# A decoder block in split fp32: plain w_down rows inside the seven-product banks, paced loads, gate/up by features

## The chip, the cores and the metric

The kernel runs on one core of one Trainium2 chip. The time is the device time of one execution in microseconds; the time before is the median of three runs, 2729.72 us (2727.82 to 2730.57). TensorE (PE) multiplies 128x128 weight tiles with a moving operand, VectorE (DVE) and ScalarE (ACT) do elementwise work. GpSimd (POOL) and SyncE (SP) here do little but issue DMAs, each on a queue of its own.

## The reference

One layer of a decoder on 512 tokens and 2048 features in fp32: attention and a gated delta rule, merged by gates, then a SwiGLU channel mixer of 5632 features and a last norm. The change touches the mixer and what follows it alone:

```python
h = _rmsnorm(x, norm_ffn[l]) * (1.0 + sc_f) + sh_f
gate, up = jnp.split(h @ w_gate_up[l], 2, axis=-1)
x = x + gt_f * ((jax.nn.silu(gate) * up) @ w_down[l])
...
return _rmsnorm(x, final_norm)
```

## The kernel before

**Precision.** Each fp32 operand is split into a high and a low part (`hi`/`lo`, `h2h`/`h2l`, `xh`/`xl`, `ah`/`al`), and each product of tiles is three matmuls: high by high, and the two mixed ones. ACT makes the high part, DVE the low one.

**Order.** Every instruction is first recorded, so that all rows of the profile show one line, L482; then a planner with costs and due times reorders DVE and ACT. PE, SP and POOL keep the order in which the program was written. A `Driver` walks through `Unit`s: a unit loads a raw weight tile (`load`, SP's queue), splits it, runs its matmuls and then a closing step. `pump` moves side chains one step on after every twelve counts; a chain that yields n rests for n−1 of its turns. `side` issues on POOL's queue. Working tiles are 68 slots of 128x512 (`S`), raw weights take a ring of five, split ones four, and PSUM has eight banks.

**Gate/up.** `w_gate_up` has 22 pairs of 256-column sets. `gu_tokens(0, ...)` and `gu_tokens(1, ...)` compute sets s=0 and 1 with token tiles as weights and 512 weight columns moving. The results have tokens on partitions, so `gu_read` applies silu and product, and later `turned_a` turns them on PE (four transposes of a block, then a copy to `f_dram`). The other 20 sets go through `strassen`, the seven-product form (`big(1)` to `big(10)`).

**w_down.** Its 44 row blocks of 128 fall into three groups. Rows 0–15 and 16–31 go through `tokens_down(ks, n)`, the seven-product form: for ks=0, 1 and n=0, 1 (1024 columns each), sixteen units; eight with the products m1, m6, m7, m5 (`FIRST4`, 24 matmuls each), then eight with m2, m4, m3 (`LAST3`, 18 each), 336 matmuls in all. The products' weights are sums of weight tiles (`sums`), stored in `s_dram` by POOL in the first eight units and loaded again in the last eight. The moving-side parts in `down[ks]` come from `f_dram` through `sums_down`. The other rows, 32–43, are plain: 36–39 stay in slots (`aT`), 32–35 and 40–43 wait in `a_dram` (`kept_a`, `reload_a`).

**The end of the program, before.** In order: gate/up s=0 and 1, the ten seven-product sets, the plain rows 36–39 for all 2048 columns (`dn(36, n)`, whose `dn_done` puts the results into `down_dram`), `tokens_down(0,0)` and `(0,1)`, the plain rows 40–43, `tokens_down(1,0)` and `(1,1)`, and the last stage `last_dn` with the plain rows 32–35, the transposed residual `x2` and the final norm. Each set's results are added to `down_dram` by adding stores on POOL (`add_down`), as a side chain that the next set finishes first: `drv.finish(chains["out"])`. In `tokens_down(1,1)`, `at(i)` names what is loaded ahead of unit i: the `down_dram` tiles (`back_s`), gate rows, x2 (`back_x`) and `a_dram` tiles (`aT_back`), the last two on POOL's queue.

Of the kernel before, what the change touches and what calls it, by code (L numbers as in the profile page):

```python
# [16 lines left out]
P = 128  # L17
T = 512
NT = 4
# [472 lines left out]
def block_kernel(ctx: ExitStack, tc: tile.TileContext, a: dict, out):  # L492
# [1805 lines left out]
    def tokens_down(ks, n):  # L2298
# [64 lines left out]
        def after(c, t):  # L2363
            tt = lambda o, x, y, op=ALU.add: nc.vector.tensor_tensor(o, x, y[:], op)
            less = lambda o, x, y: nc.vector.scalar_tensor_tensor(o, x, -1.0, y[:], op0=ALU.mult, op1=ALU.subtract)
# [10 lines left out]
            elif c == "m2":  # L2376
                if final:
                    tt(s_t[t, 2][:], s_t[t, 2][:], ps["m1"][t])
                    ps["m1"][t] = None
                    return  # L2380
                x = S("g0")
                nc.scalar.copy(x[:], ps["m1"][t][:])
                tiles[0, t, 0] = x[:]
                ps["m1"][t] = None
            elif c == "m4":
                if final:
                    tt(s_t[2 + t, 2][:], s_t[2 + t, 2][:], ps["m7"][t])
                    ps["m7"][t] = None
                    return
                x = S("g1")  # L2390
                tt(x[:], v[t], ps["m7"][t])
                tiles[1, t, 0] = x[:]
                ps["m7"][t] = None
            else:
                if final:
                    tt(s_t[t, 3][:], s_t[t, 3][:], ps["m5"][t], ALU.subtract)
# [4 lines left out]
                ps["m5"][t] = None  # L2401

# [9 lines left out]
        def outputs(keys):  # L2412
            for h, t, f in keys:
                add_down(2 * h + t, 2 * n + f, tiles.pop((h, t, f)))
                yield 2

        def unit(i):
# [5 lines left out]
            for c, w, j, bank, x in products:  # L2423
                for t in range(2):
                    for m, (xi, wi) in enumerate(((0, 0), (0, 1), (1, 0))):
                        def one(c=c, w=w, j=j, bank=bank, x=x, t=t, m=m, xi=xi, wi=wi):
                            mm(ps[bank][t][:], x(q)[xi][:, 256 * kk + P * t:256 * kk + P * t + P], box["w"][w][wi][:, j, :],
                               start=i == 0 and m == 0, stop=k == 7 and m == 2, skip_group_check=True)
# [6 lines left out]
            def post():  # L2435
# [5 lines left out]
                if i == 15:  # L2441
                    if (ks, n) == (1, 0):
                        kept.update(tiles)
                    elif not final:
                        chains["out"] = drv.add(outputs([(1, 0, 1), (1, 1, 1), (0, 0, 0), (0, 1, 0), (1, 0, 0), (1, 1, 0), (0, 0, 1), (0, 1, 1)]))
# [3 lines left out]
        return [unit(i) for i in range(16)]  # L2449

    early, s_t, rows, kept = [], {}, [], {}
    down_dram = dram.tile([NT, P, D], F32, name="down_dram")

    def add_down(t, n, src, **kw):

        nc.gpsimd.dma_start(down_dram[t][:, 512 * n:512 * n + 512], src, accum_op=ALU.add)
# [97 lines left out]
    def sums_down(ks):  # L2554
# [3 lines left out]
        def free(q):  # L2558
            return q < 4 and gone[ks] >= min(q + 2, 4) and (q < 3 or plain_sets[0] > 4 * ks + 3)
# [9 lines left out]
        for q in range(4):  # L2569
# [10 lines left out]
            for c, dst, x, y, op in (("m7", "x7", "a11", "a21", ALU.subtract), ("m1", "a11", None, None, None),  # L2580
                                     ("m5", "a21", "a22", "a21", ALU.subtract), ("m4", "a22", None, None, None),
                                     ("m6", "a11", "a11", "a21", ALU.add), ("m2", "a12", None, None, None),
                                     ("m3", "a12", "a11", "a12", ALU.subtract)):
# [18 lines left out]
    first_tiles = {}  # L2602

    def gu_read(s, ht, bank):

        if s == 0:
            first_tiles[ht] = S("g0")
        o, g = first_tiles[ht][:, 256 * s:256 * s + 256], S("sl")
        nc.scalar.activation(g[:, 0:256], bank[:, 0:256], AF.Silu)
        nc.vector.tensor_tensor(o, g[:, 0:256], bank[:, 256:512], ALU.mult)  # L2610

    def gu_tokens(s, hts):

        banks = {}

        def unit(k0):
# [8 lines left out]
            def pre():  # L2625
                if k0 == 0:
                    for ht in hts:
                        banks[ht] = PS(f"gu{s}")

            def one(kk, h, t, n, xi, wi):  # L2630
# [3 lines left out]
                if k == KT - 1 and n == 2:  # L2634
                    gu_read(s, (h, t), banks.pop((h, t)))

            mms = [lambda kk=kk, h=h, t=t, n=n, xi=xi, wi=wi: one(kk, h, t, n, xi, wi)
                   for kk in range(2) for h, t in hts for n, (xi, wi) in enumerate(((0, 0), (0, 1), (1, 0)))]

            def post():  # L2640
                if k0 + 2 == KT and s == 1:
                    for q in range(4):
                        h2T[1][q] = None
                    turning.append((0, first_tiles))

            return Unit(start, split, mms, pre, post, weight=2, alone=s == 0, late=k0 + 2 == KT)
# [3 lines left out]
    def dn_done(n, k0):  # L2650
        def done(ps):
            for t in range(NT):
                y = S("y")
                nc.scalar.copy(y[:], ps[t][:])
                if k0 == 36:
                    side(down_dram[t][:, 512 * n:512 * n + 512], y[:])
                else:
                    add_down(t, n, y[:])
            plain_sets[0] += 1
            if n == 3:  # L2660
                for k in range(k0, k0 + 4):
# [5 lines left out]
    def ffn():  # L2667
        def gu0():
            us = []
            for h in range(2):  # L2670
                half = gu_tokens(0, [(h, t) for t in range(2)])
# [5 lines left out]
                us += half  # L2677
# [6 lines left out]
            with_pre(us, start)  # L2684
            return us
# [6 lines left out]
        def dn(k1, n):  # L2692
            us = tm_set(f"dn{k1}_{n}", lambda k0, nk: plain(w_dn, k1 + k0, nk, 512 * n, 512), 4,
                        lambda k: (aT[k1 + k][0][:], aT[k1 + k][1][:]), dn_done(n, k1))
# [3 lines left out]
        LAST = 32  # L2698
# [3 lines left out]
        def load_rows(src):  # L2702
            for i in range(4):
                r = S("row")
                load(r[:], src[512 * i:512 * i + 512].partition_broadcast(P))
                rows.append(r)

        def back_x(n):
            for h in range(2):
                for q in (2 * n, 2 * n + 1):  # L2710
                    x2[h][q] = S("x2")
                    side(x2[h][q][:], x2_dram[h, q])

        def back_s(n):
            for t in range(NT):
                s_t[t, n] = S("sd")
                load(s_t[t, n][:], down_dram[t][:, 512 * n:512 * n + 512])
# [78 lines left out]
        def last_dn():  # L2796
# [4 lines left out]
            def aT_back():  # L2801
                for k in range(4):
                    reload_a(LAST + k)

            def at(i):
                if i == 2:
                    back_s(0)
                elif i == 3:
                    with_kept(0)
                    back_s(1)  # L2810
                elif i == 4:
                    with_kept(1)
                    load_rows(g_dram)
                elif i == 5:
                    gated(0)
                elif i == 6:
                    gated(1)
                    back_s(2)
                elif i == 7:
                    back_x(0)  # L2820
                elif i == 8:
                    back_s(3)
                elif i == 9:
                    early[0]()
                    back_x(1)
                elif i == 11:
                    aT_back()
                elif i == 13:
                    back_x(2)
                elif i == 14:  # L2830
                    back_x(3)
                elif i == 15:
                    load_rows(a["final_norm"])

            for i, u in enumerate(tokens_down(1, 1)):
                u = begin(lambda i=i: at(i))(u)
                yield u

            for n in range(2):
                for k0 in (0, 2):  # L2840
                    yield last_weights(n, k0)
                    for t in range(NT):
                        u = token_unit(t, n, k0=k0, nk=2, free=t == 3)
                        if k0 == 2 and t == 0:
                            u = begin(lambda n=n: gated(2 + n))(u)
# [11 lines left out]
        both = gu_tokens(1, [(h, t) for h in range(2) for t in range(2)])  # L2857
        yield from with_pre(both, lambda: xc.append(drv.add(combine())))
# [9 lines left out]
        for n in range(4):  # L2868
            for k, u in enumerate(dn(36, n)):
                yield with_pre([u], more)[0]  # L2870
                if n in (1, 2):
                    yield Unit(mms=turned_a(2 * n + k - 2), pre=lambda: drv.finish(chains["act"]))
        for n in range(2):
            for i, u in enumerate(tokens_down(0, n)):
                if (n, i) == (1, 10):
                    def start():
                        for k in range(40, 44):
                            reload_a(k)
                        maker[1] = drv.add(sums_down(1))
                    with_pre([u], start)  # L2880
                yield u
        for n in range(4):
            for u in dn(40, n):
                yield with_pre([u], more)[0]
# [64 lines left out]
```

## Time and profile before

| what | us |
|---|---|
| median of three runs (range) | 2729.72 (2727.82 to 2730.57) |
| profiled execution | 2731.62 |
| its span | 2729.8 |
| gate/up s=0 and 1 | 1375.7 to 1464.6 |
| seven-product gate/up sets | 1464.6 to 2245.2 |
| plain rows 36–39 | 2245.2 to 2290.6 |
| tokens_down(0,0) and (0,1) | 2290.6 to 2451.7 |
| plain rows 40–43 | 2451.7 to 2495.3 |
| tokens_down(1,0) and (1,1) | 2495.3 to 2669.4 |
| last stage | 2669.4 to 2720.8 |

The stages are the times from the first matmul of one to the first of the next. In a row of windows, "PE busy (x673)" has the count of matmuls behind the busy time, which is modelled; the rate is better read from the stage's length and the count. PEclk is the share of the full clock that the throttle granted. In a DMA row the last number is the median time from issue to landing.

### The profile page before, as it was taken

The page shows a single profiled execution, that of the slowest core. Times are in us where ns is not written, and L with a number is a line of the kernel's source. Part 1 is how long each engine was busy: PE and PEld are TensorE (multiplying, and loading weights), DVE is VectorE, ACT ScalarE, POOL GpSimd, SP SyncE. Part 2 cuts the span into 40 slices and gives each one's busy share as a digit, 9 for nine tenths or more (in the row PEclk, how much of TensorE's full clock was granted, in tenths as well). Part 3 has the DMA queues.
Part 4 walks back from the last instruction along what each step waited for, and adds up shares of the span by engine and source line. Part 5 has one row for each costly group of instructions (what it writes and reads, how often), then busy time and mean ns, then how long its engine had stood idle before and what let it go on. Part 6 is the DMA issues. An engine that isn't in the chain of part 4 may idle for free. (4 is left out here: it accounts for less than half of the span.)

```text
span 2729.8 us, 37437 instructions
## 1 busy us (share of the span) xinstructions
PE 2695.4 (99%) x13518; PEld 2263.3 (83%) x13518; DVE 2124.8 (78%) x3257; ACT 1181.6 (43%) x1648; POOL 230.1 (8%) x363
## 2 busy tenths in 40 slices
PE   9999999999999999999999999999999999998998
PEld 7888788888888888889988888888888888877876
DVE  8985666776978887688797777788777787876878
ACT  4343432442345343244483444444444455444434
POOL 0000011102001000000000000000000102113020
PEclk9999999999999999999999999999999999999999
DMA  9995555645666889525864566566665667689692
GB/s 345 354 369 185 164 171 165 201 137 175 187 183 214 313 291 329 193 88 126 256 199 144 192 201 204 201 212 201 204 206 189 218 217 251 198 266 211 194 347 101
DMA packets 306690, 587.13 MB, mean 215 GB/s; under 512 B 42228, under 2 KB 81412, under 8 KB 306504
## 3 DMA queue, kind: packets, MB, share of 16 engines
q1 hardware_dynamic: 260920, 481.01, 53.5%
q0 software_dynamic: 26368, 76.85, 9.4%
q10 hardware_dynamic: 19216, 26.87, 2.8%
q8 instruction: 106, 1.74, 0.3%
q14 instruction: 80, 0.66, 0.1%
HBM read 497.58 MB, written 88.09 MB: 215 GB/s over the span
## 5 line engine op out<-in xcount | busy, mean ns | idle before, releaser
L482 ACT CAST hi<-raws 128x1024 fp32r<-128x1024 f32 (+2 forms) x360 | 325.5, 905 | 546.3 <-PE m L482 274.2
L482 DVE TENSOR_TENSOR lo<-raws,hi 128x1024 fp32r<-128x1024 f32 (+2 forms) x360 | 370.2, 1039 | 169.5 <-ACT hi L482 165.1
L482 ACT CAST hi<-raw 128x1024 fp32r<-128x1024 f32 (+2 forms) x259 | 268.5, 1038 | 475.3 <-DMA raw<-in_w_in_dram 79.4
L482 DVE TENSOR_TENSOR lo<-raw,hi 128x1024 fp32r<-128x1024 f32 (+2 forms) x259 | 313.1, 1210 | 170.4 <-ACT hi L482 168.5
L482 DVE CUSTOM_DVE_ANT_0 rawm<-rawm,cbc 128x1024 f32<-128x1024 f32 x192 | 233.2, 1229 | 24.1 <-DMA rawm<-in_w_mod_dram 23.7
L482 ACT CAST hi<-sums 128x1024 fp32r<-128x1024 f32 x136 | 142.8, 1051 | 144.2 <-PE m L482 120.8
L482 DVE TENSOR_TENSOR lo<-sums,hi 128x1024 fp32r<-128x1024 f32 x136 | 166.1, 1222 | 47.2 <-ACT hi L482 46.9
L482 PE MATMUL m<-hi,h2h 128*128 128x512 f32 x480 | 190.2, 396 | 0.0
L482 PE MATMUL m<-lo,xh 128*128 128x512 f32 x448 | 178.6, 399 | 9.2 <-DVE lo L482 8.9
L482 PE MATMUL m<-hi,h2l 128*128 128x512 f32 x480 | 187.2, 390 | 0.0
L482 PE MATMUL m<-lo,h2h 128*128 128x512 f32 x480 | 187.1, 390 | 0.0
L482 PE MATMUL m<-hi,xh 128*128 128x512 f32 x448 | 177.6, 396 | 9.3 <-ACT hi L482 9.3
L482 PE MATMUL m<-hi,xl 128*128 128x512 f32 x448 | 176.8, 395 | 0.0
L482 DVE TENSOR_TENSOR sums<-raws,raws 128x1024 f32<-128x1024 f32 x112 | 136.5, 1219 | 26.2 <-DMA s_dram<-raws 23.8
L482 POOL DMA_DIRECT2D s_dram<-raws x112 | 64.1, 578 | 690.5 <-DVE raws L482 680.6
L482 PEld LDWEIGHTS m<-lo,xh 128*128 128x128 f32 x448 | 85.6, 191 | 33.2 <-DVE lo L482 15.6
L482 PEld LDWEIGHTS m<-hi,xh 128*128 128x128 f32 x448 | 85.5, 191 | 29.5 <-ACT hi L482 11.6
L482 PEld LDWEIGHTS m<-hi,h2l 128*128 128x128 f32 x480 | 90.1, 188 | 18.9
L482 PEld LDWEIGHTS m<-lo,h2h 128*128 128x128 f32 x480 | 90.3, 188 | 17.7
L482 PEld LDWEIGHTS m<-hi,h2h 128*128 128x128 f32 x480 | 90.2, 188 | 17.5
L482 PE MATMUL gb<-hh,hi 128*128 128x512 f32 x256 | 101.9, 398 | 0.0
L482 PE MATMUL gb<-hl,hi 128*128 128x512 f32 x256 | 100.0, 390 | 0.0
(538 smaller groups left out, 7026.4 us busy)
## 6 DMA issues: line engine op xcount, KB each, us to landing
raws<-in_w_gate_up_dram SPq DMA_DIRECT2D x400, 256.0 KB, 3.5
rawm<-in_w_mod_dram SPq DMA_DIRECT2D x192, 512.0 KB, 5.5
raw<-in_w_in_dram SPq DMA_DIRECT2D x143, 512.0 KB, 4.6
raws<-in_w_down_dram SPq DMA_DIRECT2D x160, 256.0 KB, 4.9
s_dram<-raws POOLq DMA_DIRECT2D x112, 256.0 KB, 3.3
raws<-s_dram SPq DMA_DIRECT2D x112, 256.0 KB, 2.8
rawa<-in_w_in_dram SPq DMA_DIRECT2D x32, 512.0 KB, 3.8
raws<-in_w_o_dram SPq DMA_DIRECT2D x48, 256.0 KB, 3.1
```

What stands on the lines that cost most here:

```text
L482: self.tc.keep_in_program_order(op.call(*op.args, **op.kwargs))
```

## The change

**Gate/up by features.** Sets s=0 and 1 now take the weight tile as the stationary operand, with 256 tokens moving: 768 matmuls of 256 columns for 384 of 512. The results have features on partitions. `gu_done` stores them to `f_dram` directly; the sixteen transposes of `turned_a` for these sets, with their copies, go. On PE, at the first stage (`gu` are PSUM banks, `hi`/`lo` the split weights, `h2h`/`h2l` the split tokens), before:

```order
L482 MATMUL gu_2138_2278<-hi_2264,h2h_2250 128x512
L482 MATMUL gu_2138_2278<-lo_2265,h2h_2250 128x512
L482 MATMUL gu_2138_2278<-hi_2264,h2l_2251 128x512
L482 MATMUL gu_2139_2279<-hi_2264,h2h_2250 128x512
L482 MATMUL gu_2139_2279<-lo_2265,h2h_2250 128x512
L482 MATMUL gu_2139_2279<-hi_2264,h2l_2251 128x512
```

and on PE at the same place after:

```order
L482 MATMUL gu_2138_2278<-h2h_2250,hi_2264 128x256
L482 MATMUL gu_2138_2278<-h2l_2251,hi_2264 128x256
L482 MATMUL gu_2138_2278<-h2h_2250,lo_2265 128x256
L482 MATMUL gu_2139_2279<-h2h_2250,hi_2264 128x256
L482 MATMUL gu_2139_2279<-h2l_2251,hi_2264 128x256
L482 MATMUL gu_2139_2279<-h2h_2250,lo_2265 128x256
```

The operands have changed places, the width is halved, and in this stage a weight tile's matmuls go to four banks, one for each block of 128 features, where they went to two, one for each block of 128 tokens.

**Plain rows.** Rows 36–39 and 32–35 are now one group of eight (`ORDER`). For columns 0–1023 they are computed in front of `tokens_down(0,0)` (`dn(0)`, `dn(1)`, 192 matmuls). For columns 1024–2047 they follow `tokens_down(0,1)` as eight `plus_unit`s, again 192 matmuls, which add into that set's own PSUM banks; `with_plus` then reads the banks out once. Rows 40–43 take the place of 32–35 in the last stage. Rows 36–39 are stored to `a_dram` too.

**down_dram.** Before, 16 tiles are put and 32 added. After, 16 are put (`put_down`) and eight added, those of `tokens_down(0,0)`, as a chain that rests between its steps; `pre` sees to it that four are out by the eighth unit of the next set and all by the sixteenth. On POOL around the first half of `tokens_down(0,1)` (`raws` is a tile of weight sums, `euvw` and `g` are result tiles), before:

```order
L482 DMA s_dram<-raws_3947 128x512
L482 DMA s_dram<-raws_3953 128x512
L482 DMA s_dram<-raws_3961 128x512
L482 DMA down_dram<-euvw 128x512 x2
L482 DMA down_dram<-g_3823_3963 128x512
L482 DMA down_dram<-g_3824_3964 128x512
L482 DMA down_dram<-g_3825_3965 128x512
L482 DMA down_dram<-g_3826_3966 128x512
L482 DMA down_dram<-euvw 128x512 x2
L482 DMA s_dram<-raws_3972 128x512
```

and on POOL at the same place after:

```order
L482 DMA s_dram<-raws_3948 128x512
L482 DMA down_dram<-euvw 128x512
L482 DMA s_dram<-raws_3963 128x512
L482 DMA down_dram<-euvw 128x512
L482 DMA s_dram<-raws_3970 128x512
L482 DMA down_dram<-euvw 128x512
L482 DMA s_dram<-raws_3977 128x512
L482 DMA down_dram<-euvw 128x512
L482 DMA s_dram<-raws_3984 128x512
L482 DMA down_dram<-g_3799_3939 128x512
L482 DMA down_dram<-g_3800_3940 128x512
L482 DMA down_dram<-g_3801_3941 128x512
```

The first four adds now stand one at a time between the stores of weight sums; the `g` adds follow the last of these.

**Paced loads.** `reload_a` moves from POOL's queue to SP's, one row block (two tiles) per unit: 32–35 in the last units of `big(10)`, all eight of `ORDER` once more in the second half of `tokens_down(0,1)`, 40–43 in the last units of `tokens_down(1,1)`. There the loads ahead of the last stage are spread too, two per unit, all on SP; twelve of the sixteen x2 loads and the final norm's rows move into the last stage (`more_back`). On POOL in the second half of `tokens_down(1,1)` before:

```order
L482 DMA s_dram<-raws_4388 128x512
L482 DMA x_4277_4417<-x_dram 128x512
L482 DMA x_4278_4418<-x_dram 128x512
L482 DMA x_4279_4419<-x_dram 128x512
L482 DMA x_4280_4420<-x_dram 128x512
L482 DMA x_4297_4437<-x_dram 128x512
```

and on SP there after:

```order
L482 DMA raws_4389<-s_dram 128x512
L482 DMA raws_4389<-in_w_down_dram 128x512
L482 DMA raws_4390<-in_w_down_dram 128x512
L482 DMA x_4251_4391<-x_dram 128x512
L482 DMA x_4252_4392<-x_dram 128x512
L482 DMA raws_4397<-s_dram 128x512
L482 DMA raws_4397<-in_w_down_dram 128x512
```

The x2 loads have left POOL's queue and stand in pairs behind each unit's three weight loads.

**Signs.** A few differences are taken the other way round (`less`, `sums_down`), one instruction for one. The diff, cut to its core:

```diff
-        else:
-            for i in range(2):
-                side(a_dram[k - 32, i], hl[i][:].bitcast(F32))
+        for i in range(2):
+            side(a_dram[k - 32, i], hl[i][:].bitcast(F32))
...
         def pre(i):
             down_ready(ks, i % 8 // 2)
+            if i == 7:
+                while "out" in chains and sent[0] < 4:
+                    drv.step(chains["out"])
+            if i == 15 and "out" in chains:
+                drv.finish(chains["out"])
             if i == 0:
                 drv.ahead = 2
-                if "out" in chains:
-                    drv.finish(chains["out"])
...
+        def with_plus(f, t):
+            if f:
+                nc.vector.tensor_tensor(v[t], ps["m5"][t][:], v[t], ALU.subtract)
+                nc.vector.tensor_tensor(up1[t], up1[t], ps["m6"][t][:], ALU.add)
+                tiles[0, t, 1], tiles[1, t, 1] = v[t], up1[t]
+                ps["m5"][t] = ps["m6"][t] = None
+            else:
+                x, y = S("g0"), S("g1")
+                nc.scalar.copy(x[:], ps["m1"][t][:])
+                nc.vector.tensor_tensor(y[:], v[t], ps["m7"][t][:], ALU.add)
+                tiles[0, t, 0], tiles[1, t, 0] = x[:], y[:]
+                ps["m1"][t] = ps["m7"][t] = None
...
+            def one(kk, t, x, w, h):
+                bank = (("m1", "m7"), ("m5", "m6"))[f][t // 2]
+                mm(ps[bank][t % 2][:], aT[plus[k0 + kk]][x][:, tok(t)], box["w"][w][:, kk, :],
+                   start=(bank, k0 + kk, h) == ("m6", 0, 0), stop=(k0 + kk, h) == (7, 2), skip_group_check=True)
+                if (k0 + kk, h) == (7, 2) and t > 1:
+                    with_plus(f, t - 2)
...
-                add_down(2 * h + t, 2 * n + f, tiles.pop((h, t, f)))
-                yield 2
+                sent[0] += 1
+                (add_down if n == 0 else put_down)(2 * h + t, 2 * n + f, tiles.pop((h, t, f)))
+                yield 5 if n == 0 else 2
...
-                mm(banks[h, t][:], half_k(h2T[h][k // 2], k)[xi][:, tok(t)], box["w"][wi][:, kk, :],
-                   start=k == 0 and n == 0, stop=k == KT - 1 and n == 2)
+                                st["ps"][j][:, 256 * h:256 * h + 256], box["w"][wi][:, kk, tok(j)], half_k(h2T[h][k // 2], k)[xi],
...
-                side(aT[k][i][:].bitcast(F32), a_dram[k - 32, i])
+                load(aT[k][i][:].bitcast(F32), a_dram[k - 32, i])
...
+        ORDER = [36, 37, 38, 39, 32, 33, 34, 35]
...
-        LAST = 32
+        LAST = 40
...
-                    side(x2[h][q][:], x2_dram[h, q])
+            load(x2[h][q][:], x2_dram[h, q])
...
+                elif i == 10:
+                    early[0]()
+                    x_back(0, 0)
+                    x_back(0, 1)
+                elif i == 11:
+                    x_back(1, 0)
+                    x_back(1, 1)
                     gated(1)
...
+                if s == 10 and i > 11:
+                    with_pre([u], lambda k=20 + i: reload_a(k))
...
+            for i, u in enumerate(tokens_down(0, n, ORDER if n else ())):
                 if (n, i) == (1, 10):
...
+                    with_pre([u], lambda: maker.__setitem__(1, drv.add(sums_down(1))))
+                if n and 8 <= i < 16:
+                    with_pre([u], lambda k=ORDER[i - 8]: reload_a(k))
                 yield u
-        for n in range(4):
-            for u in dn(40, n):
-                yield with_pre([u], more)[0]
         yield from tokens_down(1, 0)
```

More of the change, by code (lines that the diff above doesn't have):

```diff
@@ L2401, in after, with plus_unit, start, split @@
                 ps["m5"][t] = None
+        def with_plus(f, t):
[10 more added lines that the diff above has]
+                ps["m1"][t] = ps["m7"][t] = None
+        def plus_unit(f, k0):
+            box = {}
+            def start():
+                box["raw"] = fetch(plain(w_dn, plus[k0], 2, c0 + 512 * f, 512), 512, 2)
+            def split():
+                box["w"] = halves(box.pop("raw"), 512, 2)
+            def pre():
+                if (f, k0) == (1, 0):
+                    ps["m6"] = [PS("m6") for _ in range(2)]
+            def one(kk, t, x, w, h):
[4 more added lines that the diff above has]
+                    with_plus(f, t - 2)
+            mms = [lambda kk=kk, t=t, x=x, w=w, h=h: one(kk, t, x, w, h)
+                   for kk in range(2) for t in range(NT) for h, (x, w) in enumerate(((0, 0), (0, 1), (1, 0)))]
+            def post():
+                if (f, k0) == (1, 6):
+                    for k in plus:
+                        aT[k] = None
+                    plain_sets[0] += 2
+                    chains["out"] = drv.add(outputs([(1, 0, 1), (1, 1, 1), (0, 0, 1), (0, 1, 1), (0, 0, 0), (0, 1, 0), (1, 0, 0), (1, 1, 0)]))
+            return Unit(start, split, mms, pre, post, late=(f, k0) == (1, 6))
         def joins():
@@ L2654, in done @@
                 nc.scalar.copy(y[:], ps[t][:])
[L2655 to L2658, printed above, removed]
+                put_down(t, n, y[:])
             plain_sets[0] += 1
-            if n == 3:
-                for k in range(k0, k0 + 4):
+            if n % 2:
+                for k in range(32, 40):
                     aT[k] = None
@@ L2676, in gu0 @@
                     with_pre([u], ahead)
-                us += half
+                us.append(half)
             def start():
@@ L2856, in ffn @@
         yield from gu0()
-        both = gu_tokens(1, [(h, t) for h in range(2) for t in range(2)])
-        yield from with_pre(both, lambda: xc.append(drv.add(combine())))
+        yield from with_pre(gu_both(1), lambda: xc.append(drv.add(combine())))
         side(g_dram.rearrange("(k p) -> p k", p=P), gt_ffn[:])
```

225 lines of the change are left out of this document (136 added, 89 removed).

## The prediction

> **What bounds the kernel now.** I read four views in turn: the engine shares of the page, the windows of the stages that the change touches, the waits inside the longest of them, and the timeline and the DMA view at each pause. First the page:
>
> ```profile
> span 2729.8 us, 37437 instructions
> PE 2695.4 (99%) x13518; PEld 2263.3 (83%) x13518; DVE 2124.8 (78%) x3257; ACT 1181.6 (43%) x1648; POOL 230.1 (8%) x363
> ```
>
> PE is the bound; only matmul time or PE's pauses can move the end. The pace of one matmul comes from an unbroken stretch of each width: 54 steps of 512 columns in 12.24 us are 0.2267 us each, and 100 us of 256-column work hold 835 matmuls, 0.1198 us each.
>
> ```profile
> 1189.63 0.39 PE L482 MATMUL yb<-oh,lo 128*128 128x512 f32 x1
> ...
> 1201.87 0.39 PE L482 MATMUL yb<-oh,lo 128*128 128x512 f32 x1
> core 0: us, PE busy (x) PEld busy (x) DVE busy (x) ACT busy (x) POOL busy (x), PEclk, DMA share, GB/s
> 1203.00:1303.00 100.00, 100.00 (x835) 100.00 (x834) 89.99 (x137) 48.28 (x66) 9.92 (x14) 1.00 0.46 119
> 1375.70:1464.60 88.90, 88.90 (x396) 73.25 (x396) 80.22 (x128) 57.67 (x90) 1.10 (x2) 1.00 0.49 157
> 2290.60:2451.70 161.10, 156.06 (x673) 128.13 (x672) 125.84 (x148) 74.11 (x93) 22.09 (x35) 0.98 0.75 233
> 2451.70:2495.30 43.60, 43.60 (x194) 36.08 (x194) 32.91 (x44) 24.51 (x38) 15.13 (x19) 1.00 0.98 228
> 2495.30:2669.40 174.10, 160.66 (x673) 127.09 (x672) 133.39 (x160) 64.51 (x77) 25.65 (x44) 0.97 0.77 252
> 2669.40:2720.80 51.40, 51.39 (x269) 42.97 (x267) 45.32 (x82) 24.54 (x49) 0.00 (x0) 1.00 0.22 77
> 2541.00:2630.00 89.00, 89.00 (x395) 73.68 (x394) 76.02 (x92) 37.29 (x44) 13.61 (x26) 1.00 0.78 263
> ```
>
> The stages after the header are: the unbroken 256-column stretch, gate/up s=0 and 1, the two seven-product sets of rows 0–15 (672 matmuls of 512 columns), the plain rows 40–43, the two sets of rows 16–31 (again 672), the last stage, and an undisturbed piece of the fourth. At 0.2267 us, 672 matmuls need 152.3 us. So 161.1 − 152.3 = 8.8 us and 174.1 − 152.3 = 21.8 us are lost, 30.6 in all; the plain rows lose nothing (192 × 0.2267 = 43.5).
>
> Where the first loss sits and whose fault it is:
>
> ```profile
> DVE sums L482 <- DMA s_dram<-raws: 7.2, 1, 7.2
> 2373.65 1.78 POOL L482 DMA_DIRECT2D down_dram<-euvw  x2 [1.17 <-issue]
> 2374.77 4.17 POOL L482 DMA_DIRECT2D down_dram<-g  x4
> 2376.93 3.81 POOL L482 DMA_DIRECT2D down_dram<-euvw  x2
> 2379.38 1.93 POOL L482 DMA_DIRECT2D s_dram<-raws  x1
> s_dram<-raws POOLq DMA_DIRECT2D x5, 256.0 KB, 4.5
> down_dram<-g POOLq DMA_DIRECT2D x4, 256.0 KB, 10.3
> 2393.72 0.39 PE L482 MATMUL m<-hi,xl 128*128 128x512 f32 x1
> 2396.06 0.49 PE L482 MATMUL m<-hi,xh 128*128 128x512 f32 x1 [1.95 <-ACT hi L482]
> 2397.32 0.79 PE L482 MATMUL m<-lo,xh 128*128 128x512 f32 x1 [0.77 <-DVE lo L482]
> 2397.91 0.63 PE L482 MATMUL m<-hi,xl 128*128 128x512 f32 x1
> 2398.34 0.63 PE L482 MATMUL m<-hi,xh 128*128 128x512 f32 x1
> ```
>
> Eight adding stores stand in a row on POOL; the store of the weight sums behind them lands late, DVE waits 7.2 us for the raw tile that it holds, then ACT, DVE and PE are late in turn. After the pause matmuls start 0.43 us apart, not 0.23. Together about 4.5 us. The other pauses, with the loads there:
>
> ```profile
> 2424.00:2434.00 10.00, 7.68 (x27) 5.90 (x26) 6.71 (x9) 3.95 (x5) 0.00 (x0) 0.83 0.94 340
> 2510.00:2525.00 15.00, 7.85 (x25) 5.71 (x24) 8.43 (x9) 5.24 (x7) 1.98 (x3) 0.77 0.63 144
> 2630.00:2669.40 39.40, 33.87 (x126) 23.28 (x125) 27.79 (x37) 10.85 (x13) 3.73 (x7) 0.96 0.84 304
> raws<-in_w_down_dram SPq DMA_DIRECT2D x20, 256.0 KB, 4.6
> raws<-in_w_down_dram SPq DMA_DIRECT2D x14, 256.0 KB, 9.2
> down_dram<-y POOLq DMA_DIRECT2D x16, 256.0 KB, 7.7
> DMA packets 4985, 11.91 MB, mean 384 GB/s; under 512 B 725, under 2 KB 725, under 8 KB 4983
> x<-x_dram POOLq DMA_DIRECT2D x16, 256.0 KB, 7.5
> raws<-in_w_down_dram SPq DMA_DIRECT2D x9, 256.0 KB, 13.2
> sd<-down_dram SPq DMA_DIRECT2D x8, 256.0 KB, 12.2
> raws<-s_dram SPq DMA_DIRECT2D x5, 256.0 KB, 12.4
> ```
>
> The three windows are the pauses near 2424 (about 4.3 us), 2511 (9.6 us) and 2633–2667 (11.1 us; at 2537 another 1.1). The load rows: a weight load lands in 4.6 us in the calm stretch 2295–2340, in 9.2 in 2402–2430, where eight reloads from a_dram go out at once on POOL's queue, and in 13.2 in 2614–2645, where 24 loads on POOL's queue share 384 GB/s with SP's. The `y` row is of 2455–2520: the sixteen adding stores of rows 40–43 are in front of the pause at 2511.
>
> **The change part by part.** Gate/up s=0 and 1: 384 matmuls of 512 columns go (87.1 us) and 768 of 256 come (768 × 0.1198 = 92.0): **+4.9 us**, all on PE's path; that stage already runs without a gap worth naming (88.9 us). The price holds if each matmul's own weight load is hidden, as it is in 1203–1303, where 834 loads go with 835 matmuls.
>
> Sixteen transposes go. Four of them and the matmul behind:
>
> ```profile
> 1516.33 0.60 PE L482 MATMUL aT<-kc,g 128*128 128x128 f32 x4
> 1516.68 0.48 PE L482 MATMUL m<-hi,h2h 128*128 128x512 f32 x1
> 1516.99 0.39 PE L482 MATMUL m<-lo,h2h 128*128 128x512 f32 x1
> ```
>
> From 1516.33 to 1516.99 are 0.66 us for four transposes and one matmul of 0.23: 0.43 per four, so **−1.7 us** for sixteen. Their four PSUM copies on ACT, and the rewritten signs on DVE (one instruction for one), cost nothing: both engines run under the matmuls.
>
> The plain rows: the matmuls are the same in number and width (192 in front, 192 behind the second set, 192 in the last stage), so 0 on PE. For columns 1024–2047 the eight separate plain evictions go, hidden in 43.6 us without a gap. What is new is DVE's and ACT's work at the end of the second set: the next set's first weights must be ready before it. Before, 16 units of plain rows lay there with the same pattern and no loss; taken at 0.
>
> Adding stores: 32 become 8, from the first set only, in unit steps beside the weight-sum stores. The row of four `g` adds stays together behind the last weight-sum store of the set, where nothing of POOL is queued behind. So the 4.5 us near 2396 go, and so do the 9.6 at 2511 with their cause (no adds before rows 16–31).
>
> Reloads: eight a_dram tiles per group, on SP, two per unit, instead of at once on POOL. There are sixteen loads more in all and eight stores more. In the second half of set two three weight loads and two reloads are due per unit, 40 loads of 0.262 MB, and four plain tiles of 0.524 MB for the units behind: 12.6 MB. Eight units of 18 matmuls take 32.7 us, so that is 385 GB/s: just what 2614–2645 delivered. This is the tightest place. Its pause is bounded by 0 (all lands in time) and by the 4.3 us that it loses today; I take **1.5**, nearer to 0 since no burst shares the DMA engines.
>
> Set (1,1): 80 loads are due where 96 are today (48 of weights, 16 of down_dram, 4 rows, 8 of a_dram and 4 of x2 remain). With eight weight-sum stores that is 23 MB in some 81 us, 285 GB/s; 2541–2630 carries 263 without a gap. Twelve of sixteen x2 loads and half the rows move into the last stage, which moves 77 GB/s today; a load of 256 KB issued two to four units ahead has at least 24 matmuls (5.4 us) before its transposes, against 4.6 to land. Bounds 0 and 11.1; I take **1.5**, since the load per unit is now even. For set (1,0), whose first loads follow the plain units, **0.5** between 0 and 9.6. SP stays in program order: an x2 load that waits for its slot would hold back the weight loads behind it, but its slots come free 35 us before their need by the order.
>
> Sum against the profiled execution of 2731.6 us (the span and 1.8 around it): 2731.6 + 4.9 − 1.7 − 30.6 + 3.5 = 2707.7. That execution lies 1.9 above the median of the runs shown, 2729.7, so the median to expect is **2706 us**. With no pause left it would be 2702.
>
> [...] The rows above show 0.43 us spacing behind waits of 1.95 and 0.77 us. [...]
>
> **The rivals.** *Pacing only half real*: the second half of set two wants all that the DMA engines gave, so weight loads land late again, and half of the 30.6 stays. For it: 385 against 384 GB/s. Against it: 0.94 busy at 2424 came from a burst. Time: 2702 + 15.3 = 2717.
>
> *Slower: one queue for all.* In 2614–2645 SP's queue landed 22 loads in 31 us, 1.4 us apart. If that is what one queue gives, a unit with five loads takes 7.0 us where its 18 matmuls take 4.1: 2.9 us on eight units in set two, and the same in (1,1), 46 us together: 2702 + 46 = 2748. It decides once loads come more than 4.1/5 = 0.82 us apart. Against it: there POOL's queue took half of the bytes, and in 2295–2340 the queue is not the limit.
>
> *Narrow matmuls bound by weight loads.* If 384 additional loads lay bare, at the 188 ns of this row they would cost 72 us: 2706 + 72 = 2778.
>
> ```profile
> L482 PEld LDWEIGHTS m<-hi,h2l 128*128 128x128 f32 x480 | 90.1, 188 | 18.9
> ```
>
> Against it speaks 1203–1303, with the same shapes at 0.1198 us. [...]
>
> *No gain*: new pauses of 22 to 33 us take the place of the old, for instance in the gate/up stage, where two feature matmuls must wait for one split as one token matmul did: 2724 to 2735.
>
> **How the numbers follow.** The forecast with a residue of 0 to 10 us (2702 to 2712): 0.70. Half real: 0.17. Within 0.2% (5.5 us, about what a measurement of this kernel can tell from no change): 0.04. One queue: 0.07; weight loads: 0.02. Faster sums to 0.87, slower to 0.09. The range goes from 2701 (the floor less the spread of the runs) to 2720, so that the half-real case lies inside; outside stay the two slow ones, no gain, and a few in a hundred at the edges.
>
> **What would show it.** Right: gate/up near 93 us without gaps; no row of DVE waiting for s_dram above 2 us; PE gaps under 4 us in each set; no `down_dram` row in the 2500s. Wrong: PE waiting for hi or lo in the second half of set two or in (1,1) (pacing or queue), or gate/up near 160 us (weight loads). The prediction fails if SP's loads, all on one queue, land slower than a unit uses them.

## The result, and the profile after

The changed kernel takes 2698.62 us (median of four runs, 2698.45 to 2699.31) where the kernel before takes 2729.95 beside it: a ratio of 0.9887, 95% interval 0.987 to 0.9904. That is 31.3 us less; 24 were forecast, and the time lies below the stated range. The page and the windows of the changed kernel's stages, in the order of the prediction's windows:

```profile
span 2697.5 us, 38122 instructions
PE 2683.8 (99%) x13886; PEld 2277.0 (84%) x13886; DVE 2124.2 (79%) x3259; ACT 1168.9 (43%) x1620; POOL 196.7 (7%) x315
...
core 0: us, PE busy (x) PEld busy (x) DVE busy (x) ACT busy (x) POOL busy (x), PEclk, DMA share, GB/s
1369.52:1463.00 93.48, 93.48 (x781) 93.42 (x780) 80.51 (x128) 58.05 (x90) 3.36 (x5) 1.00 0.52 156
1463.00:2241.65 778.65, 778.65 (x3506) 644.81 (x3505) 615.15 (x703) 349.34 (x418) 67.14 (x124) 1.00 0.62 207
2241.65:2287.07 45.42, 45.42 (x210) 37.62 (x209) 37.55 (x50) 24.08 (x37) 8.39 (x16) 1.00 0.70 239
2287.07:2636.77 349.70, 348.86 (x1537) 288.01 (x1536) 288.74 (x348) 155.23 (x188) 29.12 (x49) 1.00 0.75 246
2636.77:2688.10 51.33, 51.33 (x269) 42.96 (x267) 45.84 (x83) 23.31 (x49) 0.00 (x0) 1.00 0.35 127
```

These are gate/up, the seven-product gate/up sets, the plain rows in front, all four seven-product sets of w_down with the plain units inside (1536 matmuls, which need 348.2 us at 0.2267), and the last stage. From the first matmul of one stage to that of the next, the 32.3 us between the two spans come from here:

| stretch | before, us | after, us | difference | forecast |
|---|---|---|---|---|
| start to the first gate/up matmul | 1375.75 | 1369.52 | −6.2 | none named |
| gate/up s=0 and 1 | 88.9 | 93.5 | +4.6 | +4.9 |
| seven-product gate/up sets | 780.5 | 778.7 | −1.9 | −1.7 |
| plain rows in front | 45.4 | 45.4 | 0 | 0 |
| from there to the last stage | 378.8 | 349.7 | −29.1 | −27.1 |
| last stage and output | 60.4 | 60.7 | +0.3 | 0 |

All that was forecast came, and within 2 us. What was not forecast is the first row: 6.2 us gained ahead of everything that the change touches. There the matmuls on PE are the same, in the same order. The kernel before has a pause in that stretch which the other lacks (timeline of PE, `hss` is the sum of squares of the norm; the first fence is of the kernel before, the second of the one after):

```profile
1354.14 1.05 PE L482 MATMUL hss<-ones,sq 128*128 128x1 f32 x8 [2.35 <-DVE sq L482]
...
1302.00:1324.00 22.00, 22.00 (x185) 22.00 (x184) 10.06 (x12) 9.51 (x12) 4.46 (x8) 1.00 1.05 221
...
raw<-in_w_o_dram SPq DMA_DIRECT2D x13, 512.0 KB, 8.2
x<-in_xT_dram SPq DMA_DIRECT2D x8, 256.0 KB, 15.1
g_dram<-gt_ffn POOLq DMA_DIRECT2D x1, 8.0 KB, 14.5
```

```profile
1349.49 0.95 PE L482 MATMUL hss<-ones,sq 128*128 128x1 f32 x8
...
1302.00:1324.00 22.00, 22.00 (x186) 22.00 (x185) 13.63 (x16) 13.48 (x18) 2.52 (x5) 1.00 1.02 355
...
raw<-in_w_o_dram SPq DMA_DIRECT2D x16, 512.0 KB, 6.7
x<-in_xT_dram SPq DMA_DIRECT2D x8, 256.0 KB, 7.3
```

Both have a full DMA share from 1302 to 1324, but one moves 221 GB/s and the other 355, and the x loads of 1290–1345 land in 15.1 us against 7.3. DVE does 12 operations there against 16, and is late when PE wants `sq`. The one transfer which the second fence lacks is `g_dram<-gt_ffn`: 8 KB, whose 2048 elements the `rearrange` sends to strided places. In the trace it is 32 packets of 256 bytes, 1310.5 to 1312.6, and in 1312–1320, right behind them, the engines move 81 GB/s where the kernel after moves 364. In the program this store is the same line behind gate/up. But POOL issues in order, and in the kernel after two `f_dram` stores of the features form stand ahead of it and wait for the gate/up results (timeline of POOL, first before, then after):

```profile
1300.75 4.66 POOL L482 DMA_DIRECT2D x<-x_dram  x8
1305.40 1.18 POOL L482 DMA_DIRECT2D g_dram<-gt_ffn  x1
...
1417.97 0.55 POOL L482 DMA_DIRECT2D f_dram<-sl  x1 [113.45 <-DVE sl L482]
1420.27 0.55 POOL L482 DMA_DIRECT2D f_dram<-sl  x1 [1.76 <-DVE sl L482]
1420.81 1.18 POOL L482 DMA_DIRECT2D g_dram<-gt_ffn  x1
```

So it goes out at 1420.8, in a stage with 156 GB/s.

### The profile page after: what moved, and what is told of

Same layout as the page of the kernel before. It is cut to its first block, busy times and chain, and to the rows that moved or that the text cites. A ratio compares the mean times of both kernels' runs of the same rounds, so it can differ in the third digit from the quotient of the medians.

```text
span 2697.5 us, 38122 instructions
## 1 busy us (share of the span) xinstructions
PE 2683.8 (99%) x13886; PEld 2277.0 (84%) x13886; DVE 2124.2 (79%) x3259; ACT 1168.9 (43%) x1620; POOL 196.7 (7%) x315
## 4 chain that ended last, share of the span: by engine, by line
PE 98%; DMA 1%; DVE 0%; ACT 0%; issue 0%; DVEq 0%; SPq 0%
PE m L482 45%; PE gb L482 7%; PE v L482 4%; PE gu L482 3%; PE z L482 3%; PE ya L482 3%; PE ga L482 3%; PE k L482 3%; PE q L482 3%; PE yb L482 3%; PE s L482 3%; PE dnt L482 2%; PE wo L482 2%; PE qk L482 2%; PE cq L482 2%; PE dn L482 2%
## 5 line engine op out<-in xcount | busy, mean ns | idle before, releaser
L482 PEld LDWEIGHTS m<-hi,h2h 128*128 128x128 f32 x480 | 90.2, 188 | 17.6
L482 PE MATMUL gb<-hh,lo 128*128 128x512 f32 x256 | 99.9, 390 | 0.0
```

The costliest lines, as they stand in the source:

```text
L482: self.tc.keep_in_program_order(op.call(*op.args, **op.kwargs))
```

## The experiments

Each was run beside the kernel before on the same chip, where that took 2731.48 (E1 to E4), 2731.54 (E5 to E8) and 2733.6 us (E9 to E12); differences below are against these. A "pause" is the time from start to start of matmuls beyond 0.2267 us each, summed over the stretch. Each kernel has one profiled execution, so a pause is read from one execution, while the times are medians.

**E1: the kernel before, its small store later.**

```diff
-        side(g_dram.rearrange("(k p) -> p k", p=P), gt_ffn[:])
...
             for i, u in enumerate(big(s)):
+                if (s, i) == (1, 4):
+                    with_pre([u], lambda: side(g_dram.rearrange("(k p) -> p k", p=P), gt_ffn[:]))
```

> The kernel before, with the one store of gt_ffn to g_dram (2048 elements of four bytes) issued on POOL's queue from unit 4 of the first seven-product set instead of right behind the x loads of the w_o stage. Nothing else is changed. Theory A (this small store lies at 1305 to 1320 us in the kernel before, fills the DMA engines with tiny packets, makes the w_o weight loads land in 15 us instead of 7, and so costs PE about 6.2 us before the gate/up stage; the change pushed it behind the new f_dram stores by accident): 2730.0 - 6.2 = 2723.7 us, gate/up starting near 1369.5 us. Theory B (the w_o stage became shorter for another reason: the planner gave DVE and ACT another order there because the gate/up stage behind it is other): 2729 to 2731 us, gate/up still starting near 1375.7.

Measured: 2731.11 us, ratio 0.9997 (0.9987 to 1.0006): by the time alone, theory B. The trace shows otherwise: gate/up starts at 1369.65, as theory A says, and 5 us are lost again behind 1464. DMA groups of 1478–1500, then DVE and PE:

```profile
raws<-s_dram SPq DMA_DIRECT2D x5, 256.0 KB, 7.0
s_dram<-raws POOLq DMA_DIRECT2D x2, 256.0 KB, 8.0
g_dram<-gt_ffn POOLq DMA_DIRECT2D x1, 8.0 KB, 11.1
...
1498.39 0.69 DVE L482 TENSOR_TENSOR raws<-raws,raws 128x512 f32<-128x512 f32 x1 [4.64 <-DMA raws<-in_w_gate_up_dram]
...
1506.79 0.79 PE L482 MATMUL m<-hi,h2h 128*128 128x512 f32 x1 [3.21 <-DVE euvw L482]
```

The store had only moved: issued at 1481.6, it makes the weight loads late that DVE needs at 1498 (in these 22 us those from w_gate_up land in 5.3 us and those from s_dram in 7.0, where the kernel before has 3.8 and 3.2). Whether its place or the shorter stage before it cost this, E5 decides.

**E2: the kernel after, its small store early.** The same line is moved to stand in front of the second half of gate/up s=0, ahead of the f_dram stores:

```diff
+            with_pre(us[1][:1], lambda: side(g_dram.rearrange("(k p) -> p k", p=P), gt_ffn[:]))
             return us[0] + us[1]
```

> The kernel after, with the store to g_dram put ahead of the f_dram stores on POOL's queue, so that it follows the x loads of the w_o stage as in the kernel before. Theory A: 2698.6 + 6.2 = 2704.8 us, gate/up starting near 1375.7. Theory B: 2698 to 2699.5 us, gate/up starting near 1369.5.

Measured: 2703.97 us, ratio 0.9896, 27.5 us less than the kernel before where the kernel after had 31.3. The timeline of PE, and the DMA groups of 1290–1345:

```profile
1353.56 1.05 PE L482 MATMUL hss<-ones,sq 128*128 128x1 f32 x8 [2.35 <-DVE sq L482]
...
x<-in_xT_dram SPq DMA_DIRECT2D x8, 256.0 KB, 15.4
...
g_dram<-gt_ffn POOLq DMA_DIRECT2D x1, 8.0 KB, 17.6
```

Gate/up starts at 1375.16, 5.6 us later than in the kernel after. Theory A holds: this one store brings the old pause back with the same 2.35 us wait for `sq` in it. All fourteen traces agree: the five with the store at 1305 start gate/up at 1375.2 to 1378.0, the nine without at 1369.2 to 1370.7.

**E3: the kernel before with gate/up by features, alone.**

```diff
-        both = gu_tokens(1, [(h, t) for h in range(2) for t in range(2)])
-        yield from with_pre(both, lambda: xc.append(drv.add(combine())))
+        yield from with_pre(gu_both(1), lambda: xc.append(drv.add(combine())))
```

(`gu0` and `gu_done` as in the kernel after.)

> The kernel before with only gate/up s=0 and 1 by features; its two first f_dram stores stand ahead of the g_dram store as in the kernel after. Theory A: -6.2 (g_dram) + 4.6 (narrow matmuls) - 1.9 (transposes): 2730.0 - 3.5 = 2726.5 us. Theory B, with the gain upstream due to this part as well: the same 2726.5. If the gain upstream came from the tail's edits (planner): 2730.0 + 2.7 = 2732.7 us.

Measured: 2727.27 us, ratio 0.9982 (0.9973 to 0.9991), 4.2 less. Gate/up starts at 1369.74 and the next stage at 1463.21. By the table of stages this edit's own work is a loss of 2.7 us (+4.6 and −1.9); the gain is the side effect on the small store, 6.0 us at the start of gate/up.

**E4: the kernel after with gate/up by tokens**, the small store as in E1.

> The kernel after with gate/up s=0 and 1 by tokens again (384 matmuls of 512 columns, sixteen transposes), and the g_dram store issued from unit 4 of the first seven-product set. Theory A: the w_o stage stays short without the features form, so 2698.6 - 4.6 + 1.9 = 2695.9 us, below both kernels. Theory B: the gain upstream belongs to the features form, so 2695.9 + 6.2 = 2702.1 us.

Measured: 2702.27 us, ratio 0.9891, theory B's number. But the start is again theory A's (gate/up at 1370.72), and the store, issued at 1482.6, costs 4.4 us behind 1500 as in E1. Where this store goes decides, which E5 and E6 test.

**E5: the kernel before, the store in a calm place**, behind the last store of the a21 tiles:

```diff
                     side(a21_dram[n, :, c], a21_)
+                    if (n, i) == (3, 7):
+                        side(g_dram.rearrange("(k p) -> p k", p=P), gt_ffn[:])
```

> The kernel before with the g_dram store issued behind the last a21 store, near 1228 us, where POOL has 14 us without work and the DMA engines move 85 GB/s. Theory A (the small store costs whatever its place delays, and nothing in a calm place): 6.2 us less than the kernel before of the same chip, so 2724 to 2725 us, gate/up starting near 1369.5 and no pause behind 1464. Rival (the second pause seen when it was issued at 1481 is a debt of the shortened w_o stage that comes due anyway): no gain, 2730 to 2731 us.

Measured: 2724.94 us, ratio 0.9975 (0.9964 to 0.9985), 6.6 less. Gate/up starts at 1370.04, and no pause comes behind 1464. The store takes 13.4 us at 1228 and the four weight loads beside it land in 11.7 (2.9 in the kernel before), but these have time. With E2 this settles the first row of the table: one line moved, in either direction, gives or takes it.

**E6: the kernel after, by tokens, the store ahead of the last gate/up unit.** Otherwise as E4:

```diff
+        with_pre(both[7:], lambda: side(g_dram.rearrange("(k p) -> p k", p=P), gt_ffn[:]))
         yield from with_pre(both, lambda: xc.append(drv.add(combine())))
```

> The kernel after with gate/up by tokens again and the g_dram store issued behind the second weight-sum store of the first seven-product set, near 1453 us (82 GB/s there, 13 us before POOL's next store). Theory A: without the pause of 4.4 us that the store made at 1481, 34 us less than the kernel before, 2.7 us less than the kernel after: near 2696 us. Rival (features form needed for the short w_o stage): 2702 us as with the store at 1481.

Measured: 2695.82 us (2695.49 to 2696.55), ratio 0.9867 (0.9852 to 0.9882): 35.7 us less than the kernel before. Windows of gate/up, of the four sets with the plain units, and of the last stage:

```profile
1370.00:1458.85 88.85, 88.85 (x397) 73.17 (x396) 80.13 (x128) 57.63 (x89) 2.26 (x3) 1.00 0.51 150
...
2284.79:2632.99 348.20, 348.20 (x1537) 288.16 (x1536) 288.40 (x348) 155.06 (x188) 29.04 (x49) 1.00 0.75 247
2632.99:2684.30 51.31, 51.31 (x269) 42.96 (x267) 45.78 (x83) 23.37 (x48) 0.00 (x0) 1.00 0.35 130
```

The store went out at 1447.9. Four weight loads beside it landed in 12.3 us, and PE did not wait for them. Gate/up is back at 88.9 us, and the 1536 matmuls take just the 348.2 us of their pace. This version is below both kernels. It did not run beside the kernel after on one chip, so the 2.8 us between them rest on two comparisons with the kernel before, and on the stages: its last stage starts 3.8 us earlier.

The other six take the 29.1 us of w_down apart. Pauses of the matmuls of the four sets in the profiled executions, us:

| kernel | 2380–2402 | 2415–2440 | 2500–2530 | 2615–2670 |
|---|---|---|---|---|
| before | 4.6 | 4.2 | 9.6 | 11.1 |
| after | 0 | 0 | 0 | 1.4 |
| E7 after, adds in a row | 5.8 | 0 | 0 | 1.2 |
| E8 after, reloads in a burst | 0 | 0 | 0 | 1.6 |
| E9 after, on POOL's queue | 0 | 0 | 0 | 2.4, and 9.0 in 2590–2615 |
| E10 before, reloads on SP | 4.7 | 0 | 9.7 | 0 |
| E11 before, last loads paced | 5.3 | 0 | 8.9 | 0.4 |
| E12 before, puts for adds | 4.4 | 0 | 4.6 | 11.0 |

**E7: the kernel after, eight adds in a row.**

```diff
-            if i == 7:
-                while "out" in chains and sent[0] < 4:
-                    drv.step(chains["out"])
-            if i == 15 and "out" in chains:
-                drv.finish(chains["out"])
             if i == 0:
                 drv.ahead = 2
+                if "out" in chains:
+                    drv.finish(chains["out"])
```

> The kernel after with the eight adding stores of the first set in a row again, at unit 0 of the second set (the chain is finished there); all else as after. Theory (the row of adds holds back the weight-sum store behind it, DVE waits for the raw tile): the pause near 2390 of about 4.5 us is back, 2698.6 + 4.5 = 2703 us. Rival (the pause came from the load of the DMA engines there, which is the same without the sixteen plain-row adds): under 1 us, 2698 to 2699.6 us.

Measured: 2705.95 us, ratio 0.9903 (0.9889 to 0.9918): 25.6 us less than the kernel before, where the kernel after had 31.3. The wait is the one of the kernel before (waits of 2370–2400):

```profile
DVE sums L482 <- DMA s_dram<-raws: 8.4, 1, 8.4
...
PE m L482 <- ACT hi L482: 3.1, 1, 3.1
```

The pause is 5.8 us. The theory holds.

**E8: the kernel after, sixteen reloads in one burst on SP.**

```diff
-                if n and 8 <= i < 16:
-                    with_pre([u], lambda k=ORDER[i - 8]: reload_a(k))
+                if (n, i) == (1, 10):
+                    with_pre([u], lambda: [reload_a(k) for k in ORDER])
```

> The kernel after with all sixteen reloads of rows 36 to 39 and 32 to 35 issued at unit 10 of the second set, in a row on SP's queue, instead of two per unit. Theory (the even spread is what lets 385 GB/s through without a pause): sixteen loads of 0.262 MB at 384 GB/s take 10.9 us in which no weight load lands, against two units (8.2 us) loaded ahead, so a pause of 3 to 11 us: 2702 to 2710 us. Rival (enough is loaded ahead): 2698 to 2699.6 us.

Measured: 2699.08 us, ratio 0.988; no pause in that half. My theory falls: the even spread is not what lets the loads through. What then? Either the queue, or nothing there was tight. E9 has these reloads on POOL's queue and no pause in that half either, so in these executions nothing there was tight.

**E9: the kernel after, the paced loads on POOL's queue.**

```diff
-                load(aT[k][i][:].bitcast(F32), a_dram[k - 32, i])
+                side(aT[k][i][:].bitcast(F32), a_dram[k - 32, i])
...
-            load(x2[h][q][:], x2_dram[h, q])
+            side(x2[h][q][:], x2_dram[h, q])
```

> The kernel after with the paced a_dram and x2 loads issued at the same places of the program, but on POOL's queue as in the kernel before. Theory Q (it is the second queue that slows the weight loads, since POOL issues far ahead of its unit as soon as a slot is free, and shares the DMA engines with SP; one queue in program order is served in the order of need): pauses of 3 to 10 us in the two second halves, 2702 to 2709 us. Theory P (it is the even spread): under 1 us, 2698 to 2699.6 us.

Measured: 2708.47 us, ratio 0.9906 (0.9889 to 0.9922). That is the time that theory Q expected. Its pauses come in one of the two second halves only: 9.8 us more than in the kernel after, at 2603 and 2613. DMA groups of 2590–2625, a wait of 2600–2622 and the pause, of E9:

```profile
x<-x_dram POOLq DMA_DIRECT2D x16, 256.0 KB, 7.3
raws<-in_w_down_dram SPq DMA_DIRECT2D x14, 256.0 KB, 7.5
...
sd<-down_dram SPq DMA_DIRECT2D x6, 256.0 KB, 10.7
...
row<-g_dram SPq DMA_DIRECT2D x2, 256.0 KB, 16.2
...
DVE raws L482 <- DMA raws<-in_w_down_dram: 12.4, 3, 7.0
...
2621.08 0.80 PE L482 MATMUL m<-lo,xh 128*128 128x512 f32 x1 [6.88 <-DVE lo L482]
```

and the same window of the kernel after:

```profile
DMA packets 6516, 12.08 MB, mean 345 GB/s; under 512 B 725, under 2 KB 725, under 8 KB 6515
...
raws<-in_w_down_dram SPq DMA_DIRECT2D x14, 256.0 KB, 5.3
sd<-down_dram SPq DMA_DIRECT2D x8, 256.0 KB, 5.3
...
x<-x_dram SPq DMA_DIRECT2D x6, 256.0 KB, 6.5
```

Sixteen x2 loads go out on POOL within these 35 us, six on SP. POOL does not keep to the pace at which SP gets on: it issues the first x2 load at 2590.2 and the first of the last a_dram reloads at 2592.4, where the kernel after has them at 2608.0 and 2618.0. The last stage wants both. On SP the weight loads then take 7.5 us for 5.3 and the rows 16.2 for 7.1, and DVE waits 7.0 us for one weight load. So the other queue changes two things, when a load is issued and what moves beside SP's loads (here 5.83 MB of POOL's queue beside 7.17 of SP's, in the kernel after 0.40 beside 11.66); these runs do not separate them.

**E10: the kernel before, bursts on SP.** The same two lines the other way in the kernel before: `side` becomes `load`, the places stay.

> The kernel before with the a_dram and x2 reloads on SP's queue, still in bursts at the old places. Theory Q: the pauses near 2424 (4.3 us) and 2633 to 2667 (11.1 us) shrink by more than half, 8 to 15 us less than the kernel before. Theory P: the bursts now stand ahead of weight loads in one queue and the pauses stay or grow: within 3 us of the kernel before, or slower.

Measured: 2718.39 us, ratio 0.9945 (0.993 to 0.996): 15.2 us less. The pause of 11.1 us is gone, with nothing paced. DMA groups of E10 in 2614–2645, where the prediction showed those of the kernel before:

```profile
raws<-in_w_down_dram SPq DMA_DIRECT2D x12, 256.0 KB, 5.4
x<-x_dram SPq DMA_DIRECT2D x12, 256.0 KB, 6.0
raws<-s_dram SPq DMA_DIRECT2D x6, 256.0 KB, 5.4
```

A weight load takes 5.4 us where it took 13.2. Theory Q holds for this stage, from both sides. The profile lacks the pause at 2424 too, but so do those of kernels that leave that place as it was.

**E11: the kernel before, last loads as in the kernel after** (`at`, `more_back`, on SP).

> The kernel before with the loads around the last stage as in the kernel after (two per unit on SP, twelve x2 loads and the final norm's rows moved into the last stage); all else as before. If the pauses of 2633 to 2667 come from these loads alone: 11 us less than the kernel before, near 2720 us on a chip where that takes 2731. If the debt of the plain rows in front feeds them too: less than 6 us gained.

Measured: 2719.64 us, ratio 0.995 (0.9935 to 0.9965): 14.0 us less, more than the 11 expected. The table has the 11.1 as 0.4. The other 3 us are not settled: this profile lacks the 4.2 at 2424, but the executions of the kernel before on this chip spread from 2730.0 to 2737.9, and one profile doesn't tell which pauses the median one had.

**E12: the kernel before, puts for adds** in rows 40–43. The additions are left out: these rows overwrite what stood in `down_dram`.

```diff
-                if k0 == 36:
+                if True:
                     side(down_dram[t][:, 512 * n:512 * n + 512], y[:])
```

> The kernel before with the sixteen adding stores of the plain rows 40 to 43 made plain stores of the same tiles. The additions are left out: these rows overwrite what earlier stages put into down_dram. If adding (10 us to land against 4.5) is what loads the DMA engines ahead of the pause near 2511: the pause of 9.6 us shrinks to under 4 us, 6 to 10 us less than the kernel before. If the number of stores or the other loads of that stage cause it: less than 2 us gained.

Measured: 2724.97 us, ratio 0.9966 (0.9953 to 0.9979), 8.6 less, of which the pause at 2511 gives 5.0 (9.6 to 4.6, where under 4 was expected). What gave the other 3.6 is not settled, as in E11. The six profiles with the adds have 8.9 to 11.3 at 2511. The waits of 2495–2530, first of the kernel before, then of E12:

```profile
DVE sums L482 <- DMA s_dram<-raws: 15.0, 2, 12.0
...
DVE sums L482 <- DMA s_dram<-raws: 6.9, 1, 6.9
```

DVE waits for the tile that a weight-sum store holds, as near 2390. Adding in these rows is about half of the cause. What keeps the other half, the eight adds of the set before or the number of stores, was not separated. In the changed kernel both are gone from there.

## Why the prediction was wrong, point by point

**The sum had no term ahead of gate/up: this is the step that failed.** The prediction held 2702 us to be the floor "with no pause left". It took the pauses of the four w_down sets for all pauses that the change could reach. On what lies ahead of gate/up it has no word: that term stood at nothing without a reason, and it was 6.2 us. The features form puts four f_dram stores on POOL's queue, two of them ahead of the store to g_dram, and I never asked what they stand in front of. E2 and E5 show 5.6 and 5.7 us at the start of gate/up by that line alone. With the store back in its old place E2 takes 2703.97 us, 2 below the forecast. So most of what the change gained beyond the forecast was luck: a store held back by accident.

**Gate/up by features, +4.9: right**, 4.6. The row of 256-column matmuls held, and the rival of bare weight loads is dead: 780 loads beside 781 matmuls in 93.5 us, with PE busy for 93.48 of them and PEld for 93.42.

**Sixteen transposes, −1.7: right**, 1.9.

**The adds in a row: right in mechanism**, E7. The pause is 4.4 to 6.6 us across the executions, not a fixed 4.5.

**The pause near 2424: wrong.** I ascribed 4.3 us to eight reloads at once on POOL's queue. It stands in the one profiled execution of the kernel before, with 2.3 us in that of E1, and not at all in those of E3, E5, E11 and E12, all of which leave that place as it was. The clock sets part of its size: in the kernel before a wait of 2.32 us ends at 2427, the matmuls of 2427.8 to 2430.8 start 0.43 us apart, and the granted clock is 0.50 in these 3 us (0.83 over 2424–2434); in E1 a wait of 2.04 us ends at 2426, the matmuls are 0.23 us apart again from 2426.3, and the clock stays at 1.00. So it is no fixed cost of that burst; how many executions have it, the runs don't tell. The sum should have carried it with a doubt.

**The pauses at 2511 and 2633: right**, and their causes too, the first in part: adding by itself is 5.0 of its 9.6 (E12), POOL's loads are all but 0.4 of the 11.1 (E10, E11).

**The residue of 3.5: too high**; 1.5 us remain, with no slow matmuls among them (granted clock 1.00 in 2287–2637). In the kernel before there are some at 2427, 0.43 us apart behind a single wait of 2.32 us. I called the second half of set two the tightest place, by 385 GB/s of demand. It lost nothing, even with the reloads in a burst (E8) or on POOL's queue (E9). The rival "one queue for all" had the sign wrong: the queue that seemed slow in 2614–2645 was slow because of the other one (weight loads of 13.2 us there, of 5.4 in E10, where SP's queue has all loads).

**Pacing** was the reason that I gave for these gains. For the stage in front of the last one, E9 and E10 show that it is the queue: bursts on SP cost nothing (0 in 2615–2670, E10), and the loads placed evenly in the program, but issued by POOL, cost 10 us. For the second half of set two, E8 and E9 show that neither mattered.

## What to carry to other kernels

When a change adds an operation to a queue that is served in order, read what stands behind it there: it is delayed too, and that can be worth more than the edit (here a store went from 1305.4 to 1420.8, and gate/up started 6.2 us earlier). Keep loads that are wanted later on the same queue as the ones wanted now, in the order of need; here a second queue issued the late ones up to 26 us earlier, and the urgent ones landed late, weight loads in 7.5 us for 5.3 (E9). And a pause in one profiled execution is a sample: look for it in a second one before it enters a sum.

## What the runs showed of the hardware that was not expected

The store of 8 KB with a strided target took 14.5 us to land in the kernel before, 9.9 in the kernel after, 11.1 in E1, 17.6 in E2 and 13.4 in E5, and what ran beside it was slow: 221 GB/s against 355 in the same 22 us, 81 against 364 in eight of them, and at 1228 weight loads of 11.7 us (E5) against 2.9 there in the kernel before. It put off gate/up by 5.7 us in the kernel before (E5). The trace has 32 packets of 256 bytes for the 2048 elements; why the store and what runs beside it are slow it does not show.

In 2614–2637 of the kernel after, all loads are on SP's queue:

```profile
DMA packets 4631, 8.52 MB, mean 371 GB/s; under 512 B 474, under 2 KB 474, under 8 KB 4630
...
x<-x_dram SPq DMA_DIRECT2D x10, 256.0 KB, 6.3
...
raws<-in_w_down_dram SPq DMA_DIRECT2D x2, 256.0 KB, 5.3
```

One queue moved 371 GB/s, and its loads landed in 5.3 to 6.5 us. With two the kernel before moved 384 in 2614–2645, 6.32 MB on POOL's queue and 5.56 on SP's; SP's loads landed in 12.2 to 13.2 us, and the pause of 11.1 us followed. How the DMA engines divide their time between two queues the traces do not show.
